# A two-layer encoder on one core: the scan's diagonal products in two column halves, one exponential per group of decays, gates per group, and priorities for the scheduler

## The chip, the cores and the metric

The kernel runs on one core of a Trainium2 chip. A core has TensorE (PE in the profile; PEld is its weight load), VectorE (DVE), ScalarE (ACT), GpSimd (POOL) and SyncE (SP, which issues the transfers). PE writes its results to PSUM tiles (128 partitions of 512 fp32 values here), from which the other engines read. The metric is the device time of one execution in microseconds; lower is better. The time before is the median of three runs, 737.57 us (736.57 to 738.35).

## What is computed

The input is x, 512 tokens of 1024 features. Layer 1 is a Mamba-2 mixer with 8 groups of 4 heads; layer 2 is differential attention with 8 heads against keys and values computed once from the residual stream; a root-mean-square norm ends it. The change lies in layer 1, whose scan is, per chunk and group:

```
acs = cumsum(a_c);  seg = acs[:, None] - acs[None, :]
decay = exp(where(causal, seg, -inf))
cb = einsum("lgn,sgn->lsg", c_c, b_c)
y_diag = einsum("lsgr,sgrp->lgrp", cb * decay, x_c)
y_off = einsum("lgn,grpn->lgrp", c_c, state) * exp(acs)
state = state * exp(acs[-1]) + einsum("lgn,lgrp->grpn", b_c, x_c * exp(acs[-1] - acs))
y = y_diag + y_off + d_skip * xs
u = y * silu(z);  u = u * rsqrt(mean(u * u) over the group) * g
x = x + u @ w_out
```

## The kernel before

All large products run as three matmuls each, of a rounded high part and the rest (`whi`, `wlo` for weights, `a_hi`, `a_lo` for activations, `yh`, `yl` for the scan's results). The weights arrive in pieces of 1 MB (`raw`); `load` issues the transfer, and the pieces of `split` turn it into `whi` on ACT and `wlo` on DVE. `fetch` lays the splits of a piece as soon as it is called, two pieces ahead of use.

Layer 1 has dense products, in the order of `order_a`: `z` (gates, four blocks of 512 features, tiles `pz`), `g` (a group's B, C and x with their convolution, tiles `pg`, `xc`), `o` (output projection, tiles `po` with `whi` and `yh`). They are written as a generator, `stream_a`; `ssd(g)` is the scan of one group and is called as soon as the dense products of that group are laid. A scheduler with a model of each instruction's time then sets the order of the instructions on every engine in layer 1, by priority and readiness; from the last rows of layer 1 on the order is that in which the code is written (`Ordered`, `T.on`), and every recorded operation has the line of that helper, L53. In layer 1 a scan's instructions therefore lie among dense matmuls wherever the scheduler put them.

The scan works on chunks of 128 tokens, NQ = 4 of them. `decays` fetches the cumulative sums of two groups in one row per head spread over all partitions (`dec`, 128 x 2048, from `acs_d`), subtracts and masks on POOL, and takes the exponentials on ACT, for the small tile `een` and for `dec` two heads at a time. Two `dec` buffers exist; `decays` for the next two groups is called within the scan of an odd group. In `ssd`, `pcb` is C times B, multiplied on DVE into `dec`; `psA` and `psB` give the states `hst`; `pyd` is the diagonal product, per chunk and head

```
T.matmul(pyd[q][:, o:o + HD], lhsT=dec[:, h, c, :], rhs=xdt[:, c, h, :], start=True, stop=True)
```

with `dec` as the 128-column stationary side and 64 columns of `xdt` as the moving side, in plain fp32. Two chunks share a PSUM tile, so a group has two batches (`pyd_0`, `pyd_1`) of eight products. `po<-hst,xc` is the part of earlier chunks. Then `dx` is summed, multiplied by the gate `zs`, squared on ACT into `tmp`, scaled on ACT by the inverse root that DVE computes (`y_y`), turned by PE (`pyt`) and split into `yh`, `yl`, which the output projection reads.

Of the kernel before, what the change touches and what calls it, by code (L numbers as in the profile page):

```python
# [9 lines left out]
F32 = mybir.dt.float32  # L10
F32R = mybir.dt.float32r
I32 = mybir.dt.int32
AF = mybir.ActivationFunctionType
ALU = mybir.AluOpType
# [3 lines left out]
P = 128  # L18
# [4 lines left out]
G = 8  # L23
R = 4
HD = 64
H = 32
NQ = 4
# [10 lines left out]

C_GA, C_GK, C_GB, C_GG, C_SG, C_DTB, C_AL, C_CB, C_CW = 0, 8, 16, 24, 40, 41, 42, 43, 75
N_PAR = 203  # L40


class Ordered:
# [18 lines left out]
def trunk(ctx, tc, x, x_t, par, w_dt, w_in, w_out, w_kvqg, w_bo, d_skip, lam_qk, fin_g, out):  # L62
    nc = tc.nc
    V, A, T = (Ordered(tc, e) for e in (nc.vector, nc.scalar, nc.tensor))
# [5 lines left out]
    small = ctx.enter_context(tc.tile_pool(name="small", bufs=2))  # L70
# [8 lines left out]
    def ss_bank(name):  # L79
        turns[0] += 1  # L80
        tag = "mm" if turns[0] % turns[1] >= 3 else "ss"
        return psum.tile([P, 512], F32, tag=tag, name=name, bufs=3 if tag == "ss" else 4)
# [14 lines left out]
    nc.scalar.dma_start(prm[:], par[:, 0:C_CB])  # L97
    prc = const.tile([P, N_PAR - C_CB], F32, name="prc")
    x_tok = res.tile([P, NT, D], F32, name="x_tok")
# [5 lines left out]
    def source(seg):  # L105
        kind, a, b = seg
        if kind == "z":
            return w_in[a * 6 + b], [prm[:, C_GA + 4 * b + i:C_GA + 4 * b + i + 1] for i in range(4)]
        if kind == "g":
            return w_in[(a // 2) * 6 + 2 + (a % 2) * 2 + b], [prm[:, C_GA + 4 * b + i:C_GA + 4 * b + i + 1] for i in range(4)]  # L110
        if kind == "o":
            return w_out[a * 2 + b], [prm[:, C_GG + 4 * a + i:C_GG + 4 * a + i + 1] for i in range(4)]
        if kind in "bc":
            return w_bo[a], None
        name = f"v{a}" if kind == "v" else a
        at = C_GK if kind in "vk" else C_GB
        return w_kvqg[[i for i in ORDER_B if i[0] not in "bc"].index(name)], [prm[:, at + i:at + i + 1] for i in range(8)]

    ready = {}
    fetched = [0]  # L120

    def load(i):

        seg = segs[i]
        src, gains = source(seg)
        nk = 8 if seg[0] in "vkqt" else 4
        w = 2048 // nk
        raw = wp.tile([P, nk, w], F32, tag="raw", name=f"raw{i}", bufs=2)
        fetched[0] += 1

        def split():

            pool, tags = (bp, ("dec", "dec")) if seg == ("o", 3, 1) else (wp, ("whi", "wlo"))
            hi, lo = (pool.tile([P, nk, w], F32R, tag=tag, name=f"{n}{i}", bufs=2) for n, tag in zip(("whi", "wlo"), tags))
            ready[seg] = (hi, lo)

            def head(k):
                if gains:
                    A.activation(hi[:, k, :], raw[:, k, :], AF.Copy, scale=gains[k])
                else:  # L140
                    A.copy(hi[:, k, :], raw[:, k, :])

            def rest(k):
                if gains:
                    V.scalar_tensor_tensor(out=lo[:, k, :], in0=raw[:, k, :], scalar=gains[k],
                                           in1=hi[:, k, :].bitcast(F32), op0=ALU.mult, op1=ALU.subtract)
                else:
                    V.tensor_tensor(out=lo[:, k, :], in0=raw[:, k, :], in1=hi[:, k, :].bitcast(F32), op=ALU.subtract)

            return [(head, rest, k) for k in range(nk)]  # L150

        if i == 0:

            nc.sync.dma_start(raw[:, 0, :], src[:, 0:w])
            for n in range(2):
                nc.sync.dma_start(xt[0][:, 0, n * 256:(n + 1) * 256], x_t[:, 0, n * 256:(n + 1) * 256])
            nc.sync.dma_start(raw[:, 1, :], src[:, w:2 * w])
            nc.sync.dma_start(xt[0][:, 1, :], x_t[:, 1, :])
            for k in range(2, 4):
                nc.sync.dma_start(raw[:, k, :], src[:, k * w:(k + 1) * w])  # L160
                nc.sync.dma_start(xt[1][:, k - 2, :], x_t[:, k, :])
            for i in range(2, 4):
                nc.sync.dma_start(xt[i], x_t[:, 2 * i:2 * i + 2, :])
            nc.sync.dma_start(prc[:], par[:, C_CB:N_PAR])
        else:
            nc.sync.dma_start(raw.rearrange("p k n -> p (k n)"), src)
        return split

    def lay(piece):
        head, rest, k = piece[:3]  # L170
        head(k)
        rest(k)

    def fetch(upto):
        while fetched[0] < min(upto, len(segs)):
            for piece in load(fetched[0])():
                lay(piece)

    def use(seg):
        fetch(segs.index(seg) + 3)  # L180
# [100 lines left out]
    def until(key):  # L281
        while key not in done:
            next(dense[0], None)
# [53 lines left out]
    bp = bctx.enter_context(tc.tile_pool(name="bp", bufs=1))  # L337
    bp2 = bctx.enter_context(tc.tile_pool(name="bp2", bufs=2))

    zt = {}  # L340
# [1 line left out]
    conv_out = {}  # L342

    def z_out(j, t, ps):
        zs = bp2.tile([P, 512], F32, tag="zs", name=f"zs{j}_{t}", bufs=6)
        A.activation(zs, ps, AF.Silu, scale=r_col[:, t:t + 1])
        zt[j, t] = zs

# [33 lines left out]
    r_col, r_row = scales("a", ss)  # L384
# [13 lines left out]
    for k in range(KD):  # L398
        w = dw[:, k].rearrange("p a b h -> p (a b h)")
# [4 lines left out]
    for c in range(NQ):  # L404
        sl, hi, lo = (slice(i * H, (i + 1) * H) for i in (c, 0, 1))
# [123 lines left out]
    bss = small.tile([P, 2, NT], F32, name="bss", bufs=1)  # L529
    decs = {}  # L530

    def decays(j):

        for g in (2 * j, 2 * j + 1):
            hs = slice(R * g, R * g + R)
            dec = bp.tile([P, R, NQ, P], F32, tag="dec", name=f"dec{g}", bufs=2)
            nc.sync.dma_start(dec.rearrange("p h c l -> p (h c l)"),
                                acs_d[hs].rearrange("h c l -> (h c l)").partition_broadcast(P))
            een = small.tile([P, R, 2], F32, tag="een", name=f"een{g}")
            GP.tensor_copy(een, dec[:, :, 1:3, P - 1])  # L540
            for h in range(R):
                GP.tensor_tensor(out=dec[:, h], in0=dec[:, h], in1=acs_tok[:, :, R * g + h].unsqueeze(2).to_broadcast([P, NQ, P]), op=ALU.subtract)
                GP.affine_select(out=dec[:, h], in_=dec[:, h], compare_op=ALU.is_ge, fill=-BIG, base=0,
                                 pattern=[[0, NQ], [1, P]], channel_multiplier=-1)
            decs[g] = (dec, een)
        for g in (2 * j, 2 * j + 1):
            dec, een = decs[g]
            A.activation(een, een, AF.Exp)
            for h in range(0, R, 2):
                A.activation(dec[:, h:h + 2], dec[:, h:h + 2], AF.Exp)  # L550

    def ssd(g):
        bc, cc, x0, x1 = conv_out.pop(g)
        xc = (x0, x1)
        dec, een = decs.pop(g)
        hs = slice(R * g, R * g + R)

        pcb = long_bank(f"pcb{g}")
# [8 lines left out]
        xdt = bp.tile([P, NQ, R, HD], F32, tag="xdt", name=f"xdt{g}")  # L567
        dx = bp.tile([P, NQ, R, HD], F32, tag="dx", name=f"dx{g}")
        for j in range(2):
            pxt = ss_bank(f"pxt{g}_{j}")  # L570
            for c in range(NQ):
# [5 lines left out]
                            in1=dsk[:, h2].unsqueeze(1).unsqueeze(3).to_broadcast([P, NQ, 2, HD]), op=ALU.mult)  # L577
# [21 lines left out]
        pyd = []  # L599
        for q in range(2):  # L600
            pyd.append(ss_bank(f"pyd{g}_{q}"))
            for c in (2 * q, 2 * q + 1):
                for h in range(R):
                    o = (c % 2) * 256 + h * HD
                    T.matmul(pyd[q][:, o:o + HD], lhsT=dec[:, h, c, :], rhs=xdt[:, c, h, :], start=True, stop=True)
            dq = dx[:, 2 * q:2 * q + 2].rearrange("p c h e -> p c (h e)")
            V.tensor_tensor(out=dq, in0=pyd[q].rearrange("p (c e) -> p c e", c=2), in1=dq, op=ALU.add)
        if g % 2 and g < G - 1:
            decays((g + 1) // 2)

        po1 = ss_bank(f"po1{g}")
        T.matmul(po1[:, 256:512], lhsT=cc[:, P:2 * P], rhs=hsf[:, 0], start=True, stop=True)
# [1 line left out]
        for c in (2, 3):  # L614
            T.matmul(po2[:, (c - 2) * 256:(c - 1) * 256], lhsT=cc[:, c * P:(c + 1) * P], rhs=hsf[:, c - 1], start=True, stop=True)
        V.tensor_tensor(out=tmp[:, 1], in0=po1[:, 256:512].rearrange("p (h e) -> p h e", e=HD),
                        in1=eacs_tok[:, 1, hs].unsqueeze(2).to_broadcast([P, R, HD]), op=ALU.mult)
        V.tensor_tensor(out=tmp[:, 2:4], in0=po2.rearrange("p (c h e) -> p c h e", h=R, e=HD),
                        in1=eacs_tok[:, 2:4, hs].unsqueeze(3).to_broadcast([P, 2, R, HD]), op=ALU.mult)
        zo = (g % 2) * 256  # L620
        u = dx.rearrange("p c h e -> p c (h e)")
        tm = tmp.rearrange("p c h e -> p c (h e)")
        for c in range(NQ):
            if c:
                GP.tensor_tensor(out=u[:, c], in0=u[:, c], in1=tm[:, c], op=ALU.add)
            V.tensor_tensor(out=u[:, c], in0=u[:, c], in1=zt[g // 2, c][:, zo:zo + 256], op=ALU.mult)
            A.activation(tm[:, c], u[:, c], AF.Square, accum_out=ss4[:, c:c + 1])
        v4 = small.tile([P, NQ], F32, tag="v4", name=f"v4{g}")
        V.tensor_scalar(out=v4, in0=ss4, scalar1=ROOT2 / 256.0, scalar2=ROOT2 * EPS, op0=ALU.mult, op1=ALU.add)
# [10 lines left out]
            V.tensor_tensor(out=yl[:, j, :], in0=pyt, in1=yh[:, j, :].bitcast(F32), op=ALU.subtract)  # L640
        yT[g] = (yh, yl)

    decays(0)
    dense[0] = stream_a()
    for g in range(G):
        until(f"g{g}")
        ssd(g)
    until("o3")


# [336 lines left out]
    h = DH - 1  # L987
# [59 lines left out]
    y, f, o, dst = half(3, 0)  # L1047
# [71 lines left out]
```

## Time and profile before

| | |
|---|---|
| median of three runs | 737.57 us |
| profiled execution | 736.51 us |
| its span | 734.7 us |
| granted TensorE clock | 0.998 |
| PE busy | 723.1 us (98%) |
| PEld busy | 605.0 us (82%) |
| DVE busy | 530.8 us (72%) |
| ACT busy | 445.3 us (61%) |
| POOL busy | 114.8 us (16%) |

Busy time is the time in which at least one instruction of the engine ran. A matmul's row shows its length from entering the array to leaving it, and matmuls overlap, so what one costs is the distance between starts. "Idle before" is the engine's idle time ahead of an instruction, put down to what ended it. The chain of work that ended last is followed back from the last instruction, and says at each moment what the end of the execution hung on; in its pieces, an ACT piece without a name is the load of a function table.

### The profile page before, as it was taken

What the parts mean: (1) busy time and instruction counts of PE and PEld (TensorE: products, weight loads), DVE (VectorE), ACT (ScalarE), POOL (GpSimd) and SP (SyncE); (2) the same over time, 40 slices, a digit from 0 to 9 for tenths busy, and PEclk for the clock granted to TensorE, in tenths of its full rate; (3) what the DMA queues carried; (4) which work ended last, traced back from release to release, by engine and by line L of the source; (5) the groups of instructions that cost most, each with busy time, mean ns of one, the idle gap of its engine ahead of it and who ended that gap; (6) DMA issues with size and microseconds to landing.
All of it is one profiled execution on the core that took longest, in us unless ns stands there. A gap on an engine that the chain in (4) does not pass through costs nothing.

```text
span 734.7 us, 10327 instructions
## 1 busy us (share of the span) xinstructions
PE 723.1 (98%) x3733; PEld 605.0 (82%) x3733; DVE 530.8 (72%) x1202; ACT 445.3 (61%) x975; POOL 114.8 (16%) x158
## 2 busy tenths in 40 slices
PE   9999999999999999999999999999999999999996
PEld 7788878888887888877888879888898898889874
DVE  5679955798568669469895655666757857785886
ACT  6849672864829356256433258766766766766566
POOL 0117231402233141150110201000000000000002
PEclk9999999999999999999999999999999999999999
DMA  8552313224132233132113220331221131122003
GB/s 314 215 193 97 128 45 116 78 95 172 59 114 65 108 115 116 58 116 102 71 58 114 87 86 8 115 115 58 65 109 57 58 116 58 58 80 93 29 1 114
DMA packets 12914, 70.83 MB, mean 96 GB/s; under 512 B 1728, under 2 KB 2496, under 8 KB 5312
## 3 DMA queue, kind: packets, MB, share of 16 engines
q1 hardware_dynamic: 12576, 69.90, 26.5%
q8 instruction: 29, 0.48, 0.3%
q10 hardware_dynamic: 288, 0.28, 0.1%
q14 instruction: 21, 0.17, 0.1%
HBM read 68.02 MB, written 2.16 MB: 96 GB/s over the span
## 4 chain that ended last, share of the span: by engine, by line
PE 86%; DVE 6%; ACT 5%; issue 1%; DMA 1%; POOL 0%; ACTq 0%; POOLq 0%; SPq 0%
PE pg L53 20%; PE po L53 13%; PE pz L53 10%; PE pt L53 7%; PE pv L53 6%; PE pq L53 6%; PE pk L53 6%; PE pyd L53 4%; PE pb L53 3%; PE sc L53 3%; PE pc L53 2%; DVE wlo L53 2%; ACT L53 1%; PE pyt L53 1%; PE pxt L53 1%
## 5 line engine op out<-in xcount | busy, mean ns | idle before, releaser
L53 DVE SCALAR_TENSOR_TENSOR wlo<-raw,prm,whi 128x512 fp32r<-128x512 f32 (+1 forms) x256 | 151.4, 640 | 49.6 <-ACT whi L53 49.2
L53 ACT ACTIVATE whi<-raw,prm 128x512 fp32r<-128x512 f32 (+1 forms) x256 | 137.1, 609 | 58.5 <-PE pz L53 12.4
L53 PE MATMUL pg<-a_hi,whi 128*128 128x512 f32 x256 | 102.4, 401 | 0.4 <-DVE xc L53 0.4
L53 PE MATMUL pg<-a_hi,wlo 128*128 128x512 f32 x256 | 102.7, 404 | 0.0
L53 PE MATMUL pg<-a_lo,whi 128*128 128x512 f32 x256 | 101.4, 397 | 0.0
L53 DVE SCALAR_TENSOR_TENSOR xc<-pg,prc,xc 128x511 f32<-128x511 f32 (+2 forms) x96 | 70.0, 743 | 4.4 <-ACT xc L53 3.6
L53 PEld LDWEIGHTS pg<-a_hi,whi 128*128 128x128 f32 x256 | 48.2, 188 | 11.4 <-issue 0.8
L53 PEld LDWEIGHTS pg<-a_hi,wlo 128*128 128x128 f32 x256 | 48.1, 188 | 11.0
L53 PEld LDWEIGHTS pg<-a_lo,whi 128*128 128x128 f32 x256 | 48.2, 188 | 10.8
L53 PE MATMUL po<-whi,yh 128*128 128x512 f32 x128 | 50.9, 400 | 0.7 <-ACT yh L53 0.6
L53 PE MATMUL po<-wlo,yh 128*128 128x512 f32 x128 | 50.9, 400 | 0.4 <-DVE wlo L53 0.4
L53 PE MATMUL pz<-wlo,a_hi 128*128 128x512 f32 x128 | 50.5, 401 | 0.0
L53 PE MATMUL pz<-whi,a_lo 128*128 128x512 f32 x128 | 50.1, 399 | 0.0
L53 PE MATMUL po<-whi,yl 128*128 128x512 f32 x128 | 49.9, 396 | 0.0
L53 PE MATMUL pz<-whi,a_hi 128*128 128x512 f32 x128 | 49.6, 400 | 0.0
L53 ACT ACT_TABLE_LOAD x33 | 42.3, 1283 | 9.5 <-DVE xc L53 7.9
L957 POOL TENSOR_TENSOR ot<-ot,fg 128x512 f32<-128x512 f32 x4 | 5.1, 1285 | 257.6 <-PE pc L53 256.4
L53 ACT ACTIVATE s<-s,mx 128x128 f32<-128x128 f32 (+3 forms) x64 | 35.6, 559 | 9.5 <-DVE mx L53 9.3
L580 POOL TENSOR_TENSOR xe<-xdt,tok 128x256 f32<-128x256 f32 x24 | 15.4, 672 | 152.5 <-DVE xdt L53 152.5
L53 DVE CUSTOM_DVE_ANT_0 s<-sc,bias 128x128 f32<-128x128 f32 (+3 forms) x64 | 29.4, 488 | 12.3 <-PE sc L53 11.9
L53 PE MATMUL pv<-whi,b_hi 128*128 128x256 f32 x128 | 36.6, 286 | 0.0
L53 ACT ACTIVATE tmp<-dx 128x256 f32<-128x256 f32 x32 | 13.1, 411 | 38.0 <-DVE dx L53 38.0
(244 smaller groups left out, 1749.1 us busy)
## 6 DMA issues: line engine op xcount, KB each, us to landing
raw<-in_w_in SPq DMA_DIRECT2D x23, 1024.0 KB, 4.9
raw<-in_w_kvqg SPq DMA_DIRECT2D x16, 1024.0 KB, 4.8
dec<-acs_d SPq DMA_DIRECT2D x8, 1024.0 KB, 4.8
raw<-in_w_out SPq DMA_DIRECT2D x8, 1024.0 KB, 4.7
raw<-in_w_bo SPq DMA_DIRECT2D x4, 1024.0 KB, 4.8
x_tok<-in_x SPq DMA_DIRECT2D x4, 512.0 KB, 9.4
out<-ot SPq DMA_DIRECT2D x7, 256.0 KB, 2.4
raw<-in_w_in SPq DMA_DIRECT2D x4, 256.0 KB, 5.4
```

What stands on the lines that cost most here:

```text
L53: i = op(*args, **kw)
L580: GP.tensor_tensor(out=xe[:, c], in0=xdt[:, c], in1=toe_tok[:, c, hs].unsqueeze(2).to_broadcast([P, R, HD]), op=ALU.mult)
L957: GP.tensor_tensor(out=o, in0=o, in1=f, op=ALU.mult)
```

## The change

The diagonal product of a chunk and head is issued as two matmuls, one for output rows 0 to 63 and one for 64 to 127, each with 64 columns of `dec` as the stationary side. `dec` and `een` become one tile of 2056 columns, whose exponential is one instruction per group; `decays` takes a list of groups. The gates are written as tiles of 256 columns, one per group. The splits that `fetch` lays, and the whole scan of the last group, are laid under `tc.high_priority()`.

```diff
+N_DEC = R * NQ * P + 2 * R
...
     def fetch(upto):
         while fetched[0] < min(upto, len(segs)):
-            for piece in load(fetched[0])():
-                lay(piece)
+            pieces_ = load(fetched[0])()
+            with tc.high_priority():
+                for piece in pieces_:
+                    lay(piece)
...
     def z_out(j, t, ps):
-        zs = bp2.tile([P, 512], F32, tag="zs", name=f"zs{j}_{t}", bufs=6)
-        A.activation(zs, ps, AF.Silu, scale=r_col[:, t:t + 1])
-        zt[j, t] = zs
+        for i in range(2):
+            zs = bp2.tile([P, 256], F32, tag="zs", name=f"zs{j}_{t}_{i}", bufs=12)
+            A.activation(zs, ps[:, i * 256:(i + 1) * 256], AF.Silu, scale=r_col[:, t:t + 1])
+            zt[2 * j + i, t] = zs
...
-    def decays(j):
-        for g in (2 * j, 2 * j + 1):
+    def decays(gs):
+        for g in gs:
...
-            dec = bp.tile([P, R, NQ, P], F32, tag="dec", name=f"dec{g}", bufs=2)
+            both = bp.tile([P, N_DEC], F32, tag="dec", name=f"dec{g}", bufs=2)
+            dec = both[:, 0:R * NQ * P].rearrange("p (h c l) -> p h c l", h=R, c=NQ)
+            een = both[:, R * NQ * P:].rearrange("p (h q) -> p h q", h=R)
...
-            een = small.tile([P, R, 2], F32, tag="een", name=f"een{g}")
...
-        for g in (2 * j, 2 * j + 1):
-            dec, een = decs[g]
-            A.activation(een, een, AF.Exp)
-            for h in range(0, R, 2):
-                A.activation(dec[:, h:h + 2], dec[:, h:h + 2], AF.Exp)
+        for g in gs:
+            A.activation(decs[g][2], decs[g][2], AF.Exp)
...
-                    T.matmul(pyd[q][:, o:o + HD], lhsT=dec[:, h, c, :], rhs=xdt[:, c, h, :], start=True, stop=True)
+                    for r in (slice(0, 64), slice(64, 128)):
+                        T.matmul(pyd[q][r, o:o + HD], lhsT=dec[:, h, c, r], rhs=xdt[:, c, h, :], start=True, stop=True)
...
-            V.tensor_tensor(out=u[:, c], in0=u[:, c], in1=zt[g // 2, c][:, zo:zo + 256], op=ALU.mult)
+            V.tensor_tensor(out=u[:, c], in0=u[:, c], in1=zt[g, c], op=ALU.mult)
...
-        ssd(g)
+        if g < G - 1:
+            ssd(g)
+        else:
+            with tc.high_priority():
+                ssd(g)
```

The scheduler orders layer 1 anew, so rows move on every engine. On PE, around the first batch of group 0, before:

```order
L53 MATMUL psA_697<-xe_688,bt_670 128x256
L53 MATMUL psB_703<-xe_688,bt_670 128x256
L53 MATMUL pyd_0_709<-xdt_672,dec_444 128x64 x8
L53 MATMUL pg_2_644<-a_hi,whi_556 128x512
L53 MATMUL pg_2_644<-a_lo,whi_556 128x512
```

and now:

```order
L55 MATMUL psA_699<-xe_690,bt_672 128x256
L55 MATMUL psB_705<-xe_690,bt_672 128x256
L55 MATMUL pyd_0_711<-xdt_674,dec_452 64x64 x16
L55 MATMUL pg_2_646<-a_hi,whi_558 128x512
L55 MATMUL pg_2_646<-a_lo,whi_558 128x512
```

Here the place is the same, and eight products of 128 output rows have become sixteen of 64; in all eight groups the two batches stay apart, with full-width matmuls between.

On ACT, between the squares of group 0 and the scaling of its `tmp`, with the exponentials of group 2 (`een`, `dec`), before:

```order
L53 ACT_TABLE_LOAD
L53 ACTIVATE een_1003<-een_1003 128x8
L53 ACTIVATE tmp_708,ss_707<-dx_673 128x256 x2
L53 ACT_TABLE_LOAD
L53 ACTIVATE xc_907<-xc_907 128x512
L53 ACTIVATE tmp_708,ss_707<-dx_673 128x256
L53 ACT_TABLE_LOAD
L53 ACTIVATE dec_1001<-dec_1001 128x1024 x2
L53 ACT_TABLE_LOAD
L53 ACTIVATE zs_0_1168<-pz_0_914,ar_col 128x512
L53 ACTIVATE tmp_708<-dx_673,y_y 128x256 x4
```

and now:

```order
L55 ACTIVATE xc_925<-xc_925 128x512
L55 ACTIVATE tmp_710,ss_709<-dx_675 128x256 x2
L55 ACT_TABLE_LOAD
L55 ACTIVATE dec_1035<-dec_1035 128x2056
L55 ACT_TABLE_LOAD
L55 ACTIVATE zs_0_0_1196<-pz_0_932,ar_col 128x256
L55 ACTIVATE zs_0_1_1198<-pz_0_932,ar_col 128x256
L55 ACTIVATE tmp_710<-dx_675,y_y 128x256 x4
```

Four table loads have become two here; in the whole program 33 have become 23.

On ACT, in the scan of the last group, from its state (`hst`) to the parts of its result (`yh`), before:

```order
L53 ACTIVATE whi_3474<-raw_3472,prm 128x512 x4
L53 COPY hst_3267<-psA_3268 128x256
L53 ACTIVATE tmp_3279,ss_3278<-dx_3244 128x256 x3
L53 ACTIVATE whi_3610<-raw_3608,prm 128x256 x2
L53 ACTIVATE tmp_3279,ss_3278<-dx_3244 128x256
L53 ACTIVATE whi_3610<-raw_3608,prm 128x256 x6
L53 ACTIVATE tmp_3279<-dx_3244,y_y 128x256 x4
L53 CAST yh_3336<-pyt_0_3338 128x512
```

and now:

```order
L55 ACTIVATE whi_3610<-raw_3608,prm 128x512 x4
L55 COPY hst_3387<-psA_3388 128x256
L55 ACTIVATE tmp_3399,ss_3398<-dx_3364 128x256 x3
L55 ACTIVATE whi_3746<-raw_3744,prm 128x256 x5
L55 ACTIVATE tmp_3399,ss_3398<-dx_3364 128x256
L55 ACTIVATE whi_3746<-raw_3744,prm 128x256 x3
L55 ACTIVATE tmp_3399<-dx_3364,y_y 128x256 x4
L55 CAST yh_3472<-pyt_0_3474 128x512
```

Three of the splits have moved ahead of the last square; their number between the third square and the scaling is the same.

More of the change, by code (lines that the diff above doesn't have):

```diff
@@ L133, in split @@
             pool, tags = (bp, ("dec", "dec")) if seg == ("o", 3, 1) else (wp, ("whi", "wlo"))
-            hi, lo = (pool.tile([P, nk, w], F32R, tag=tag, name=f"{n}{i}", bufs=2) for n, tag in zip(("whi", "wlo"), tags))
+            if pool is bp:
+                hi, lo = (pool.tile([P, N_DEC], F32R, tag=tag, name=f"{n}{i}", bufs=2)[:, 0:2048].rearrange("p (k n) -> p k n", k=nk)
+                          for n, tag in zip(("whi", "wlo"), tags))
+            else:
+                hi, lo = (pool.tile([P, nk, w], F32R, tag=tag, name=f"{n}{i}", bufs=2) for n, tag in zip(("whi", "wlo"), tags))
             ready[seg] = (hi, lo)
@@ L530, in trunk @@
     decs = {}
-    def decays(j):
-        for g in (2 * j, 2 * j + 1):
+    def decays(gs):
+        for g in gs:
             hs = slice(R * g, R * g + R)
-            dec = bp.tile([P, R, NQ, P], F32, tag="dec", name=f"dec{g}", bufs=2)
-            nc.sync.dma_start(dec.rearrange("p h c l -> p (h c l)"),
+            both = bp.tile([P, N_DEC], F32, tag="dec", name=f"dec{g}", bufs=2)
+            dec = both[:, 0:R * NQ * P].rearrange("p (h c l) -> p h c l", h=R, c=NQ)
+            een = both[:, R * NQ * P:].rearrange("p (h q) -> p h q", h=R)
+            nc.sync.dma_start(both[:, 0:R * NQ * P],
                                 acs_d[hs].rearrange("h c l -> (h c l)").partition_broadcast(P))
-            een = small.tile([P, R, 2], F32, tag="een", name=f"een{g}")
             GP.tensor_copy(een, dec[:, :, 1:3, P - 1])
@@ L544, in decays @@
                                  pattern=[[0, NQ], [1, P]], channel_multiplier=-1)
-            decs[g] = (dec, een)
-        for g in (2 * j, 2 * j + 1):
-            dec, een = decs[g]
-            A.activation(een, een, AF.Exp)
-            for h in range(0, R, 2):
-                A.activation(dec[:, h:h + 2], dec[:, h:h + 2], AF.Exp)
+            decs[g] = (dec, een, both)
+        for g in gs:
+            A.activation(decs[g][2], decs[g][2], AF.Exp)
     def ssd(g):
@@ L554, in ssd @@
         xc = (x0, x1)
-        dec, een = decs.pop(g)
+        dec, een, _ = decs.pop(g)
         hs = slice(R * g, R * g + R)
@@ L608, in ssd @@
         if g % 2 and g < G - 1:
-            decays((g + 1) // 2)
+            decays((g + 1, g + 2))
         po1 = ss_bank(f"po1{g}")
@@ L619, in ssd @@
                         in1=eacs_tok[:, 2:4, hs].unsqueeze(3).to_broadcast([P, 2, R, HD]), op=ALU.mult)
-        zo = (g % 2) * 256
         u = dx.rearrange("p c h e -> p c (h e)")
@@ L641, in ssd @@
         yT[g] = (yh, yl)
-    decays(0)
+    decays((0, 1))
     dense[0] = stream_a()
@@ L646, in trunk @@
         until(f"g{g}")
-        ssd(g)
+        if g < G - 1:
+            ssd(g)
+        else:
+            with tc.high_priority():
+                ssd(g)
     until("o3")
```

## The prediction

> **What bounds the kernel now.** I read the page first: how busy each engine is, and which engine the chain that ended last runs along.
>
> ```profile
> span 734.7 us, 10327 instructions
> PE 723.1 (98%) x3733; PEld 605.0 (82%) x3733; DVE 530.8 (72%) x1202; ACT 445.3 (61%) x975; POOL 114.8 (16%) x158
> PE 86%; DVE 6%; ACT 5%; issue 1%; DMA 1%; POOL 0%; ACTq 0%; POOLq 0%; SPq 0%
> ```
>
> PE is busy almost all the time, and 86% of the chain is PE. So time comes off in two ways only: PE's own instructions get shorter, or PE's few waits go. The profiled execution took 736.5 us for a span of 734.7, 1.1 under the median of the three runs shown (737.6); the sum below is made against 736.5 and carried to the median at the end.
>
> Next, the product that the change splits, in the view of one tile, and the chain from 70 to 130 us, where it lies on the path.
>
> ```profile
> L53 PEld LDWEIGHTS pyd<-xdt,dec x256: 187/192/192, 76.5 to 415.9; 128*128 128x128 f32 x128
> L53 PE MATMUL pyd<-xdt,dec x256: 217/275/275, 76.7 to 416.0; 128*128 128x64 f32 x128
> ...
> 75.31 0.43 PE psA L53 x2
> ...
> 76.83 1.73 PE pyd L53 x16
> 78.56 4.95 PE pg L53 x21
> 83.51 1.75 PE pyd L53 x16
> ```
>
> Each fp32 product is two passes (128 products, 256 loads and 256 matmuls). A batch of eight products, 16 passes, holds PE for 1.73 us, so a pass costs 0.108 us; the 275 ns of the tile's row are a length in the pipe, not a price. There are 16 batches: 16 x 1.73 = 27.7 us of the span. What sets 0.108? The moving side has 64 columns. A psA pass moves 256 columns of fp32 and costs 0.43/2 = 0.215, so 64 columns at that rate are 0.054. The stationary side has 128 columns in either case. The score matmuls of the second layer show this apart, in a type of one pass:
>
> ```profile
> 542.51 0.27 PE L53 MATMUL sc<-k,q_lo 128*128 128x128 f32 x1
> 542.63 0.27 PE L53 MATMUL sc<-k,q 128*128 128x128 f32 x1
> 542.74 0.27 PE L53 MATMUL sc<-k,q_lo 128*128 128x128 f32 x1
> ...
> 548.98 0.28 PE L53 MATMUL sc<-k,q_lo 128*128 128x256 f32 x1
> 549.10 0.28 PE L53 MATMUL sc<-k,q 128*128 128x256 f32 x1
> 549.22 0.28 PE L53 MATMUL sc<-k,q_lo 128*128 128x256 f32 x1
> ```
>
> The first number is the start. Passes of 256 columns start 0.12 apart (half of the 4.95/21 = 0.236 of the 512-column passes pg above), but passes of 128 columns still start 0.11 to 0.12 apart and not 0.06. What they share is the 128-column weight load. So a pass with few columns is paced by its load at about 0.11, and half of PE's time in pyd is spent loading.
>
> Last, PE's waits, and what ACT does ahead of one of them.
>
> ```profile
> PEld pyt L53 <- ACT tmp L53: 4.4, 13, 1.1
> PEld po L53 <- ACT yh L53: 0.8, 1, 0.8
> ...
> 99.27 1.28 ACT L53
> 100.55 0.01 issue
> 100.56 2.01 ACT dec L53 x2
> 102.57 0.02 issue
> 102.59 1.28 ACT L53
> ...
> 104.47 1.71 ACT tmp L53 x4
> 106.17 0.04 issue
> 106.22 0.55 PE pyt L53 x3
> ```
>
> The transposes pyt wait for the scaled tmp, 4.4 us in 13 places over all groups. At 98 to 106 us the chain leaves PE: ACT loads a function table (the unnamed 1.28), takes the decays' exponentials, loads a table back, and only then scales tmp.
>
> **The change part by part.**
>
> *Column halves.* 128 products become 256 of 64 output rows, each two passes: 512 loads of 64 columns and 512 matmuls in place of 256 and 256. No row of this trace has a tile narrower than 128 columns, so the price of a pair of half passes is bounded. From below: both halves side by side, 0.054, the moving side's rate. From above: each half as dear as a whole one, 2 x 0.108 = 0.216. Between them stands 0.108: loads of 64 columns at half the time, one after the other. I take 0.060, next to the moving rate, because the halves have different output partitions and different weights and no value passes between them; the 0.006 on top is my allowance, since the rows show no fixed cost per pass. 256 x (0.108 - 0.060) = 12.3 us less. At 0.054 it is 13.8 less, at 0.108 nothing, at 0.216 27.7 more.
>
> The Trainium skill ("TensorEngine Tiling (Array Packing)", Key Properties) says that different tiles can load weights and multiply in parallel, which by itself would bring the pair to 0.054; the trace before has no tiles to show it.
>
> *Entering and leaving the halves.* There are 16 batches, so 32 changes of tile shape, each beside a full-width product. No row shows one. Nearest is the first full-width pass behind a batch:
>
> ```profile
> 76.67 1.89 PE L53 MATMUL pyd<-xdt,dec 128*128 128x64 f32 x16
> 78.37 0.48 PE L53 MATMUL pg<-a_hi,whi 128*128 128x512 f32 x1
> 78.68 0.40 PE L53 MATMUL pg<-a_lo,whi 128*128 128x512 f32 x1
> 78.92 0.40 PE L53 MATMUL pg<-a_hi,wlo 128*128 128x512 f32 x1
> ```
>
> It holds PE 0.31 against 0.24 for the next: 0.07 for a load that nothing long enough hid. If the array had to empty at each change, a pass's length less its moving time (0.275 - 0.054 = 0.22) and a load (0.11) would show: 0.33. So a change costs 0 to 0.33, 0 to 10.6 us in all. I take 0.15, nearer to the row than to the bound: 32 x 0.15 = 4.8 us more.
>
> The Trainium skill, in the same page and section, also says that a change of tiling mode drains the engine; by that, with the 0.33 of an emptied array, this term would be 10.6 and the two terms together -1.7.
>
> *Exponentials in one instruction, gates in halves, and the order.* These rows are ACT's.
>
> ```profile
> L53 ACT ACT_TABLE_LOAD x33 | 42.3, 1283 | 9.5 <-DVE xc L53 7.9 <-PEq L1112 1.2
> L53 ACT ACTIVATE dec<-dec 128x1024 f32<-128x1024 f32 x16 | 16.6, 1055 | 1.1 <-POOL dec L543 1.0
> L53 ACT ACTIVATE tmp<-dx 128x256 f32<-128x256 f32 x32 | 13.1, 411 | 38.0 <-DVE dx L53 38.0
> L53 ACT ACTIVATE zs<-pz,ar_col 128x512 f32<-128x512 f32 x16 | 10.6, 678 | 1.4 <-PE pz L53 1.3
> ```
>
> One exponential over 2056 columns instead of two over 1024 is within 0.2 us of the 2.01 that two take. What changes is the order: no een stands alone before a second table, and the built program holds 23 table loads where the old one holds 33, so 10 x 1.28 = 12.8 us of ACT go. Gates in halves add 16 instructions: two of some 0.5 (between the 0.41 of a 128x256 and the 0.68) for one of 0.68, 16 x 0.3 = 5 us more on ACT. Both lie beside PE, with ACT 61% busy; if that cover went, they would net to 8 us less on ACT. They count where PE waits for ACT. The splits laid ahead of other work and the last scan's priority likewise move only who goes first on ACT and DVE; no transfer is added, and from the last row sums of the first layer on, ACT and DVE have the same rows as before. So the gain here is bounded by the waits of pyt and po, 4.4 + 0.8 = 5.2. The exponentials with their tables no longer stand between the squares and the scaling at 98 to 106 us in parts, but one load pair still does, and the last scan still has eight splits between its squares and its scaling. I take 2.0 less, 0 to 5.2, and as a new wait at worst 4 more: the scan's steps have less PE work beside them when batches are shorter.
>
> Sum: -12.3 + 4.8 - 2.0 = -9.5; 736.5 - 9.5 = 727.0, and against the median 737.6 - 9.5 = 728.1. I say 728.
>
> **The rivals.**
>
> *Loads in turn, and the changes of shape paid (slower).* The two halves use all 128 rows of the array and their loads go through one port, one after the other. For it: every load in this trace covers 128 columns and paces the short passes, and nothing shows two loads at once. Against it: the halves are independent. Then a pair costs 0.108, the gain is nothing and the changes remain: 0 + 4.8 - 2.0 = +2.8, 740; at 0.22 a change, +5, 743. It decides from a pair price of 0.097 on, where 256 x 0.011 = 2.8 no longer pays. The Trainium skill ("TensorE: Matmul & The Clock Gate", the mechanism of Part 3) sees a load overlap a running matmul only when the row group differs, and column halves share all rows: by that rule this rival holds.
>
> *The halves do nothing.* Loads in turn, and a change of shape as cheap as 0: only the 2.0 of waits go, or none of them: 736 to 738.
>
> *The gain given back as waits.* Halves at 0.060, but pyt and po wait longer, since PE reaches them 1.5 us sooner in each group (2 x (1.73 - 0.96)): +4 in place of -2.0 gives -3.5, 734. Against it stands DVE at 72%.
>
> *Each half as dear as a whole.* +27.7 + 4.8 - 2.0 = +30.5, 768. For it: the 0.11 could be the floor of any pass and not the time of its load, since every load in this trace has 128 columns and no row can part the two. Against it stands only that a load half as wide moves half as much.
>
> **How the numbers follow.** Side by side with net gain 0.58; loads in turn with a price 0.20; nothing 0.09; given back 0.08; as dear as two 0.05. The low end is the pair at 0.054 (-13.8), changes at 0.05 (1.6) and most of the waits gone (-4.4): 737.6 - 16.6 = 721. The high end is 743, loads in turn at 0.22 a change. Only the last case and tails lie outside. The likeliest case alone spans 721 to 735. 0.2% (1.5 us) is about what a measurement of this kernel can tell from no change. Faster: 0.58, most of given back (0.06) and a little of nothing (0.02) make 0.66; same: the rest of nothing and a little of the others, 0.08; slower: 0.26.
>
> **What would show it.** The chain's pyd pieces, 16 passes in 1.73 now: 32 half passes in about 1.0 if side by side, 1.7 if in turn, 3.5 if each is whole. The first full-width pass behind a batch: 0.31 now, 0.4 to 0.65 if the array empties. Table loads: 23. PE's waits for tmp: under 4.4 in all. Wrong would make it, above all, a pair price that stays at 0.108, or a price of shape changes at its upper bound.

## The result and the profile after

The changed kernel takes 729.12 us in the median of four runs (727.83 to 730.13) against 737.11 before (four runs, the three given above and one more); the ratio is 0.9887, 95% interval 0.9874 to 0.9900. The profiled execution has a span of 727.0 us, 7.7 under that of before. These are the same rows of the page of the changed kernel: span, busy time, the chain by engine.

```profile
span 727.0 us, 10819 instructions
PE 713.5 (98%) x3989; PEld 593.1 (82%) x3989; DVE 528.0 (73%) x1202; ACT 433.7 (60%) x965; POOL 117.7 (16%) x158
PE 90%; DVE 7%; ACT 1%; issue 1%; POOL 0%; ACTq 0%; DVEq 0%; POOLq 0%
```

PE has 256 matmuls more and is busy 9.6 us less. The chain hangs on PE as before, and ACT's share of it has gone from 5% to 1%.

The split product, in the groups of its tile (the load above, the pass below; the mean ns of one is among the columns), then in the chain around group 0 (start, length, engine, tile), then on PE's timeline:

```profile
L55 PEld LDWEIGHTS pyd<-xdt,dec x512: 132/138/138, 78.2 to 408.3; 128*64 128x64 f32 x171
L55 PE MATMUL pyd<-xdt,dec x512: 222/222/270, 78.2 to 408.4; 128*64 128x64 f32 x171
```

```profile
77.88 0.43 PE psB L55 x2
78.31 1.08 PE pyd L55 x32
79.39 5.10 PE pg L55 x21
84.49 1.08 PE pyd L55 x32
```

```profile
77.72 0.59 PE L55 MATMUL psB<-xe,bt 128*128 128x256 f32 x2
78.24 1.15 PE L55 MATMUL pyd<-xdt,dec 128*64 128x64 f32 x32
79.33 0.50 PE L55 MATMUL pg<-a_hi,whi 128*128 128x512 f32 x1
79.66 0.40 PE L55 MATMUL pg<-a_lo,whi 128*128 128x512 f32 x1
```

Twice the instructions take 1.08 us in place of 1.73. Within a batch a half pass starts 0.030 us after the last one on average (from the starts of all 16 batches), so a pair of halves costs 0.060. The single starts show the pairs: the second half starts 0.007 after the first, and the next pair 0.052 after that, so in the steady part a pair costs 0.0585. Whole passes started 0.112 apart there. The rest of the average is at the ends of a batch: the second pair comes 0.05 late, and from the last half pass to the first full-width one 0.15 go by. That first pg pass holds PE for 0.33, where it held it for 0.31 before, and not for the 0.4 to 0.65 that the prediction gives an emptied array. At the entry, psB's second pass is followed 0.09 later than its own 0.215.

The waits of PE and of its weight loads that changed most (who waited for whom, us in total, times, longest), and ACT's rows that changed:

```profile
PE pg L55 <- DVE y_c L55: 1.5, 1, 1.5
...
PE po L55 <- DVE xc L55: 0.8, 1, 0.8
PE pyt L55 <- ACT tmp L55: 0.7, 1, 0.7
PE pxt L55 <- ACT xc L55: 0.6, 1, 0.6
...
PEld pyt L55 <- ACT tmp L55: 1.8, 4, 1.2
```

```profile
L55 ACT ACT_TABLE_LOAD x23 | 29.5, 1283 | 6.8 <-DVE xc L55 3.0 <-DVE y_c L55 2.4 <-PEq L1126 1.2
...
L55 ACT ACTIVATE dec<-dec 128x2056 f32<-128x2056 f32 x8 | 15.4, 1924 | 7.7 <-POOL dec L554 7.6
...
L55 ACT ACTIVATE zs<-pz,ar_col 128x256 f32<-128x256 f32 x32 | 12.9, 472 | 0.1
```

The waits of pyt for the scaled tmp fell from 4.4 us in 13 places to 1.8 in 4. Others came: before a pg matmul (1.5), a po (0.8), a pxt (0.6). The largest is late because of DVE, as the chain around it shows.

```profile
322.92 0.61 DVE pg L55
323.53 0.34 DVE v L55
...
323.89 0.98 DVE y_i L55
...
324.90 0.99 DVE y_y L55
...
325.91 0.56 DVE y_c L55
...
329.16 1.32 DVE xc L55 x2
330.47 0.08 DVE y_c L55
...
330.62 2.57 PE pg L55 x10
```

DVE works off a scan's root (v, y_i, y_y, y_c) between the steps of a convolution (pg, xc), and the pg matmul waits for them. The wait is put down to y_c because it ended last; a pg matmul reads no y_c, so what it needed was more likely the xc step just ahead of it, which the root had made late.

To tell the two causes apart I added up, for every kernel, the distances between starts on PE. "Batches" is what the pyd batches hold, from the first start to the next full-width matmul, with what the matmul before and the one behind take beyond their usual distance. "Waits" is what all other distances exceed the usual ones (0.233 for 512 columns, 0.117 for 256, 0.215 for 256 in fp32, 0.109 for 128), the start of the program included and the 7.0 to 7.1 us behind the last product left out.

| kernel | median us | ratio to before, interval | span | batches | waits |
|---|---|---|---|---|---|
| before | 737.1 | | 734.7 | 28.6 | 10.9 |
| changed | 729.1 | 0.9887 (0.9874 to 0.9900) | 727.0 | 20.5 | 11.2 |
| e1 whole products | 743.5 | 1.0085 (1.0071 to 1.0099) | 742.0 | 28.6 | 18.1 |
| e2 halves alone | 745.0 | 1.0098 (1.0080 to 1.0117) | 740.4 | 20.5 | 24.7 |
| e3 halves by side | 742.3 | 1.0079 (1.0063 to 1.0096) | 738.3 | 32.5 | 10.6 |
| e4 joined by the scheduler | 733.3 | 0.9950 (0.9936 to 0.9963) | 730.7 | 26.1 | 9.3 |
| e5 joined and kept | 722.8 | 0.9806 (0.9791 to 0.9821) | 720.9 | 17.7 | 7.9 |
| e6 quarters | 734.8 | 0.9971 (0.9959 to 0.9982) | 732.0 | 19.7 | 17.0 |
| e7 no scan priority | 731.4 | 0.9927 (0.9906 to 0.9948) | 728.3 | 20.5 | 12.5 |
| e8 no priority | 732.1 | 0.9937 (0.9919 to 0.9954) | 730.8 | 20.5 | 15.0 |
| e9 two exponentials | 730.6 | 0.9912 (0.9891 to 0.9932) | 727.9 | 20.5 | 12.1 |
| e10 wide gates | 739.0 | 1.0030 (1.0016 to 1.0044) | 737.6 | 20.8 | 21.5 |

All other products are the same in every kernel, so the spans differ as the two columns do: 734.7 - 727.0 = 7.7 is 8.1 from the batches less 0.3 more of waits. "Waits" is what is left over, and holds more than idle time. In five kernels PE worked for a while at a granted clock of 0.50 (half clock, below) in the middle of the program, and I put the passes' excess there at about 2.8 us of the column in e1, 3.0 in e2, 1.5 in e6, 2.7 in e8 and 3.9 in e10. The other seven have no such stretch before their last product. The five with it are the five with the most waits; the last section returns to this.

### The profile page after: what moved, and what is told of

Read it like the earlier page. It is cut to its first block, busy times and chain, and to the rows that moved or that the text cites. A ratio compares the mean times of both kernels' runs of the same rounds, so it can differ in the third digit from the quotient of the medians.

```text
span 727.0 us, 10819 instructions
## 1 busy us (share of the span) xinstructions
PE 713.5 (98%) x3989; PEld 593.1 (82%) x3989; DVE 528.0 (73%) x1202; ACT 433.7 (60%) x965; POOL 117.7 (16%) x158
## 4 chain that ended last, share of the span: by engine, by line
PE 90%; DVE 7%; ACT 1%; issue 1%; POOL 0%; ACTq 0%; DVEq 0%; POOLq 0%
PE pg L55 21%; PE po L55 14%; PE pz L55 12%; PE pt L55 7%; PE pv L55 6%; PE pq L55 6%; PE pk L55 6%; PE pb L55 3%; PE sc L55 3%; PE pyd L55 2%; PE pc L55 2%; DVE wlo L55 2%; DVE xc L55 2%; PE pyt L55 1%; PE pxt L55 1%; PE psA L55 1%
## 5 line engine op out<-in xcount | busy, mean ns | idle before, releaser
L55 ACT ACTIVATE xc<-pg,prc 128x512 f32<-128x512 f32 x32 | 24.6, 773 | 26.6 <-DVE pg L55 26.5
L589 POOL TENSOR_TENSOR xe<-xdt,tok 128x256 f32<-128x256 f32 x24 | 17.3, 749 | 139.6 <-DVE xdt L55 139.6
L55 ACT ACTIVATE xc<-xc 128x512 f32<-128x512 f32 x32 | 20.0, 629 | 28.3 <-DVE xc L55 28.2
```

The source lines that it names most:

```text
L55: i = op(*args, **kw)
L589: GP.tensor_tensor(out=xe[:, c], in0=xdt[:, c], in1=toe_tok[:, c, hs].unsqueeze(2).to_broadcast([P, R, HD]), op=ALU.mult)
```

## The experiments

**e1: the products whole again.**

```diff
-                    for r in (slice(0, 64), slice(64, 128)):
-                        T.matmul(pyd[q][r, o:o + HD], lhsT=dec[:, h, c, r], rhs=xdt[:, c, h, :], start=True, stop=True)
+                    T.matmul(pyd[q][:, o:o + HD], lhsT=dec[:, h, c, :], rhs=xdt[:, c, h, :], start=True, stop=True)
```

> The changed kernel with the diagonal products whole again (128 columns of dec stationary), all its other edits kept. Theory (the halves carry the gain: 16 batches of 1.08 us go back to 1.72, entries and exits of 0.25 a batch go): +8.1 us on the changed kernel, about 737, a batch of 16 passes at 1.70 to 1.73. Rival (the new order and the fewer table loads carry it): 729 to 731.

743.46 us, 6 us over what the theory had, and the rival's 729 to 731 fails too. The batches are back at 28.6, 8.1 more, as expected; a batch in the chain of this kernel:

```profile
77.15 0.43 PE psB L55 x2
77.58 1.73 PE pyd L55 x16
79.31 4.49 PE pg L55 x19
```

But the waits rose by 6.9 as well, some 2.8 of it at half clock. The scheduler orders layer 1 anew when the products change, and this order is worse. So the other edits without the halves made a kernel slower than before.

**e2: the kernel before with the halves alone.**

> The kernel before with the column halves alone. Theory (halves carry all, the other edits about nothing): 737.1 - 8.1 = 729, with 1.5 us either way for waits, since the scheduler orders layer 1 anew; a batch at 1.08. Rival (the halves pay only together with the other edits' order): 733 or more.

744.95 us: the theory's 729 failed. The batches fell by 8.1 to 20.5, the same as in the changed kernel; the waits went from 10.9 to 24.7. One of them, from this kernel's waits, then on PE's timeline:

```profile
PE po L53 <- DVE x_tok L53: 6.3, 1, 6.3
```

```profile
229.97 0.40 PE L53 MATMUL po<-whi,yl 128*128 128x512 f32 x1
236.69 0.79 PE L53 MATMUL po<-whi,yh 128*128 128x512 f32 x1 [6.33 <-DVE x_tok L53]
237.29 0.63 PE L53 MATMUL po<-wlo,yh 128*128 128x512 f32 x1
```

The gain of the halves is in the trace in full, and one order of the rest takes it back nearly twice over. The rival's 733 or more came true, and by the waits, not by the price of a half. So neither e1 nor e2 shows a gain by itself; that the halves carry it rests on the batches, which fall by the same 8.1 in both comparisons.

**e3: the same halves, sixteen of one side and then sixteen of the other.**

```diff
-            for c in (2 * q, 2 * q + 1):
-                for h in range(R):
-                    o = (c % 2) * 256 + h * HD
-                    for r in (slice(0, 64), slice(64, 128)):
+            for r in (slice(0, 64), slice(64, 128)):
+                for c in (2 * q, 2 * q + 1):
+                    for h in range(R):
+                        o = (c % 2) * 256 + h * HD
```

> The changed kernel with the loop over halves outermost in a batch: sixteen passes on the lower 64 output rows, then sixteen on the upper, so neighbours in the row use the same half of the array. Same products, same number of instructions. Theory (two halves run side by side only when neighbours are on different halves of the array; one half alone is held to its moving rate, 0.054 a pass): 32 x 0.054 + 0.12 = 1.85 a batch, 16 x 0.77 = +12.3 us on the changed kernel, about 741. Rival (a load and a pass of half width are simply cheaper, 0.030, wherever they go): a batch stays at 1.08 and the kernel at 729.

742.28 us, the theory's 741 within its scatter. The chain of this kernel:

```profile
77.45 1.83 PE pyd L55 x32
...
84.37 1.83 PE pyd L55 x32
```

1.83 a batch (1.85 expected), 12.0 more over all batches, and the order around it is nearly that of the changed kernel, with waits of 10.6. On one side half passes start 0.058 to 0.059 apart, as far as whole pairs do in the changed kernel. The average is 0.054, because at the change of side three pairs start 0.004 to 0.006 apart; the trace does not say why these ran together. Same instructions, same load widths: only that neighbours use the two sides in turn makes two half passes start in the time of one. This shows that the two halves run side by side, loads included, and that a smaller load by itself brings nothing here (1.83 against 1.73 for whole products).

**e4: both batches of a group behind each other, by PSUM tile.**

```diff
+        pyd = [ss_bank(f"pyd{g}_0"), long_bank(f"pyd{g}_1")]
         for q in range(2):
-            pyd.append(ss_bank(f"pyd{g}_{q}"))
             for c in (2 * q, 2 * q + 1):
...
+        for q in range(2):
             dq = dx[:, 2 * q:2 * q + 2].rearrange("p c h e -> p c (h e)")
```

> The changed kernel with the second batch of a group in the PSUM tile of pcb, so that both batches stand behind each other on PE: 16 changes of tile shape fewer. Theory (a change costs 0.125 us): -2.0 us, 727, where no new wait comes; a double batch of 64 half passes at 0.030 = 1.92 + 0.12. Rival (the cost at the ends of a batch is the pipe's and not the shape's, or the sums that follow come late): 729 or more.

733.31 us. The kernel was not what the expectation assumed: the scheduler issued products as soon as a head of dec was ready, and PE's chain shows them in pieces among psA and psB:

```profile
75.16 0.27 PE pyd L55 x4
75.43 0.63 PE psA L55 x2
...
76.94 0.27 PE pyd L55 x4
77.21 0.63 PE psB L55 x2
77.84 1.55 PE pyd L55 x46
```

That is 29 visits to the halves instead of 16 (a visit is an unbroken row of half passes on PE); 5.6 us more in the batches, 0.43 for each extra visit (two psA passes take 0.63 among them, 0.43 elsewhere). It measured the price it was to save, from the other side. The rival's 729 or more came true for a third reason.

**e5: joined, and the sixteen products kept in their order.**

```diff
+        pyd = [long_bank(f"pyd{g}_0"), ss_bank(f"pyd{g}_1")]
+        T.on = True
         for q in range(2):
...
                         T.matmul(pyd[q][r, o:o + HD], lhsT=dec[:, h, c, r], rhs=xdt[:, c, h, :], start=True, stop=True)
+        T.on = False
+        for q in range(2):
```

> The changed kernel with the first batch in the PSUM tile of pcb (free only when all four heads of dec are multiplied) and the sixteen products of a group kept in their order on PE, so that the 64 half passes of a group stand together: 8 visits to the halves instead of 16. Theory (a visit costs 0.26 us net, two changes of shape at 0.13): 8 x 0.26 = 2.1 us less PE time in the batches and their ends; 727 if the other waits stay. Rival (a visit's price is in the tail of the last pass and grows with the batch): no change in the batches, 729.

722.76 us, the fastest here: 0.9806 of before (0.9791 to 0.9821), with the changed kernel at 0.9887. Its chain (the span is 720.9):

```profile
77.69 0.43 PE psB L55 x2
78.12 2.02 PE pyd L55 x64
80.14 1.13 PE pg L55 x4
```

8 visits of 2.02 in place of 16 of 1.08: the batches with their ends go from 20.5 to 17.7, 2.8 us for 8 visits fewer, 0.35 a visit. That bears the theory out (2.1 expected), and the rival falls. The other 3.3 us are waits, 7.9 in place of 11.2; they come with the new order and are not credited to the joining. That is why it came out 4 us below the theory's 727.

**e6: quarters of 32 rows** (four slices in the loop over r).

> The changed kernel with each product in four parts of 32 output rows. Theory A (the moving side at 0.054 is the bound, any number of column parts runs side by side): four quarter passes in 0.054 to 0.060, a batch of 64 in 1.0 to 1.1, 729. Theory B (the 0.030 from one half pass to the next is a least distance between passes): 64 x 0.030 + 0.12 = 2.04 a batch, 16 x 0.96 = +15 us, about 744.

734.82 us: neither number. The batch itself decides clearly. Its row in the chain of this kernel:

```profile
78.65 1.03 PE pyd L55 x64
```

64 quarter passes in 1.03, 0.014 apart, four in 0.056. So theory A holds for the array: the 0.060 of a pair is the moving side's, not a least distance between passes nor a load's length, since loads of half the columns leave it where it was. Four parts bring next to nothing over two because the moving side was already the bound. The span is 5.0 over the changed kernel's: 0.8 less in the batches, 5.8 more in waits (17.0), one of 3.5 before a pcb matmul.

**e7 and e8: no priority for the last scan; none at all.**

```diff
-        if g < G - 1:
-            ssd(g)
-        else:
-            with tc.high_priority():
-                ssd(g)
+        ssd(g)
```

(e8 also lays the splits in `fetch` without priority.)

> The changed kernel without the priority of the last scan. Theory (the scheduler's order around 360 to 430 us decides PE's waits there, now 1.0 before a po matmul at 361 and 0.9 + 0.7 at 420 to 424): a change of under 1 us either way, 728 to 730. Rival (the priority holds back the splits and causes the 1.0): 728 or less, with that wait gone.

> The changed kernel without either priority (splits, last scan). Theory (the priorities are what keeps PE's waits at 12.9 us in all, where halves alone on the kernel before had 26.3): waits of 20 us or more, 735 or more. Rival (the waits come from the exponentials and their table loads, which stay as in the changed kernel): 729 to 731.

731.44 and 732.05 us: e7 lies 1.4 over its theory and e8 well under its own, 1 over its rival. The batches are unchanged. Without the scan's priority the wait before the last pyt grows from 0.9 to 1.9 and the wait at 361 stays, so the priority did not cause that one; the effect, 1.3 of span, is at the edge of what these runs can tell. Without both, waits are 15.0, not 20, so the priorities are not what keeps the kernel from e2's 24.7 (26.3 in the expectation, which used an earlier count, with 12.9 for the 11.2). They are worth some 2 to 3 us here, but e8's 15.0 hold 2.7 of half clock behind a wait that e7 has as well, without half clock.

**e9: the exponentials as before, in the tiles of the change.**

```diff
-            A.activation(decs[g][2], decs[g][2], AF.Exp)
+            dec, een, both = decs[g]
+            A.activation(een, een, AF.Exp)
+            for h in range(0, R, 2):
+                A.activation(dec[:, h:h + 2], dec[:, h:h + 2], AF.Exp)
```

> The changed kernel with the exponentials as before, een alone and dec in two, in the tiles of the change: 31 table loads instead of 23. Theory (the new waits of PE come from the order that the scheduler happens to find and not from ACT's work; the pyt waits at 98 to 106 us come back): 8 x 1.28 = 10 us more on ACT, of which PE sees 1 to 3 in new waits: 730 to 732. Rival (ACT's time is hidden beside PE): 729.

730.55 us, waits 12.1, span 0.9 longer. The intervals of this kernel and the changed one overlap, so between the theory's 730 and the rival's 729 it does not decide; it shows that eight table loads more (31 in its trace) cost at most 1 or 2 us in the order they brought.

**e10: gates in tiles of 512, read in halves.**

> The changed kernel with the gates in tiles of 512 as before, read in halves. Theory (5 us less of ACT work, all beside PE; what moves is the order): the halves as in the changed kernel, waits of PE between 9 and 19 us in all, 726 to 735. Rival (the gates per group pay by themselves, as half the tile comes free a group sooner): 731 or more with waits for the gates before pz.

738.96 us, beyond the theory's 735. The largest waits of this kernel:

```profile
PE po L55 <- DVE xc L55: 4.3, 1, 4.3
PE pg L55 <- DVE xc L55: 2.7, 1, 2.7
```

They are DVE's convolution steps. In its list of waits a gate ends one only, 0.2 us of a weight load for pg; a wait of 1.5 before pz is put down to DVE. So the rival's mechanism is not there either, though its 731 or more came true: the edit that takes ACT work away made the kernel 10 us slower by another order, some 3.9 of it at half clock. (The batches are 20.8 because one is issued in two parts.)

## Why the prediction was right

The mechanism was right: the halves run side by side, changing over costs a few us, and what is left is 8.1 us of PE's own time.

*Column halves, -12.3.* 512 half passes at 0.030 are 15.4, against 27.7: 12.3. The 0.060 for a pair was taken by reasoning from the moving rate; e3 and e6 show that this is what it is. The rival "loads in turn" is excluded by the pair's 0.060, "as dear as two" by the 1.08.

The Trainium skill ("TensorEngine Tiling (Array Packing)", Key Properties) has tiles load and multiply in parallel; the trace agrees, 0.060 a pair and 0.056 for four quarters. The Trainium skill's rule on row groups ("TensorE: Matmul & The Clock Gate", the mechanism of Part 3), by which loads of column halves would not overlap running matmuls, does not hold here: loads 138 ns long start 7 and 52 ns apart in turn, while passes of the other half run.

*Changes of shape, +4.8.* Batches and ends beyond the passes themselves are 20.5 - 15.4 = 5.1 now and 28.6 - 27.7 = 0.9 before: 4.2, or 0.13 for each of 32 changes, with 0.15 taken. How the 8.1 divides depends on the count. By the steady distances, 0.112 a pass before and 0.0585 a pair now, the passes fall by 13.7 and the ends grow by 5.6, which is 0.35 for each of 16 visits. e5, which takes 8 visits away, measures the same 0.35, and e4, which adds 13, measures 0.43. The sum does not depend on the count: -8.1, with -7.5 forecast. That the price is one of visits is shown.

*Waits, -2.0.* This is the term that was mis-sized: it measured +0.3. Its first half was right (pyt's waits went from 4.4 to 1.8, table loads from 33 to 23). What it missed is that the scheduler's new order brings waits of its own, for DVE, of the same size. The bound of 4 us for new waits was also too small for the step as a whole: among kernels with the same batches, to 0.3 us, the waits run from 11.2 to 24.7 (e2, e7 to e10 and the changed one). The changed kernel has the least of these six, and nothing in the prediction could tell that it would; that 729.1 came so near to 728 is in this part luck. The rival "the gain given back as waits" is what e2 and e10 did, mostly by waits for DVE ahead of po and pg.

*ACT.* Tables -12.8 and gates +5 were to net -8; ACT fell 11.6. The gates cost 12.9 - 10.6 = 2.3 in busy time: two of 0.47 for one of 0.68 would be 4.2 more over all, but the two overlap on ACT (32 of 0.47 are 15.1 us, busy for 12.9). The exponentials took 1.2 less.

## What to carry to other kernels

A product with few moving columns (64 here) is paced by its 128-column weight load, 0.112 a pass; cut in two column halves that alternate on PE, it falls to its moving rate, 0.0585 a pair, and it must be in turn, not side after side. Each visit to the halves costs 0.35 to 0.43 us here, so keep such products together, if need be by fixing their order. Where a scheduler orders the work, judge an edit by PE's instructions and by PE's waits separately: here the waits moved by up to 14 us for edits that touched PE not at all or for the better.

## What the runs showed of the hardware

*A long wait can cost twice.* These are stretches of e2 around its 6.3 us wait (length, PE, PEld, DVE, ACT, POOL busy, then granted clock, DMA share, GB/s):

```profile
225.00:230.00 5.00, 5.00 (x23) 3.97 (x22) 5.00 (x7) 4.99 (x9) 4.60 (x6) 1.00 0.28 80
...
236.00:240.00 4.00, 3.31 (x8) 2.63 (x9) 3.90 (x12) 2.02 (x3) 0.00 (x0) 0.50 0.69 262
```

After the wait the granted clock was 0.50 until 240.5 us, and 512-column passes started 0.42 apart (237.29 and 237.71). The length of the wait does not decide it alone. In e1 a wait of 2.3 us at 141 was followed by 3.4 us at half clock, in e3 one of 2.4 us at 337 by none. In e8 and e7 PE waits at the same place, 1.8 us (e8) and 1.9 us (e7) before the last pyt and 0.8 and 0.7 behind it. These are the 6.5 us that follow, of e8 and then of e7:

```profile
424.00:430.50 6.50, 6.04 (x15) 4.53 (x16) 1.29 (x2) 1.07 (x2) 0.00 (x0) 0.50 0.02 6
```

```profile
424.00:430.50 6.50, 5.93 (x26) 4.64 (x26) 1.55 (x3) 1.07 (x2) 0.00 (x0) 1.00 0.07 28
```

PE issues 15 passes at half clock where it issues 26 at the full one. All stretches at half clock before the last product are 3.41 or 6.83 us long in these traces. The Trainium skill ("TensorE: Matmul & The Clock Gate", What's actually happening) explains this by a free-running window of activity of 3.4 us, with half clock after at least one idle window; the traces agree with the length, but the waits of 1.8 and 2.3 us are shorter than such a window. So a wait of some 2 us can cost up to 3 us more behind it, or nothing; no trace here tells beforehand which.

*POOL slows small DVE instructions.* An instruction of POOL in the changed kernel, on its timeline:

```profile
320.94 4.92 POOL L553 TENSOR_TENSOR dec<-dec,tok 128x512 f32<-128x512 f32 x4
```

DVE's steps of a scan's root on 128x4 values on the timeline of the same kernel, two that begin within that instruction (320.94 to 325.86) and two later ones that are clear of POOL:

```profile
323.89 0.97 DVE L55 TENSOR_SCALAR y_i<-v 128x4 int32<-128x4 int32 x1
324.90 0.98 DVE L55 TENSOR_SCALAR y_y<-y_i 128x4 int32<-128x4 int32 x1
...
420.31 0.16 DVE L55 TENSOR_TENSOR y_c<-y_y,v 128x4 f32<-128x4 f32 x1
420.51 0.16 DVE L55 TENSOR_TENSOR y_c<-y_c,y_y 128x4 f32<-128x4 f32 x1
```

In the changed kernel 14 of the 80 such steps start while POOL works on dec and take 0.55 in the median, the 65 clear of POOL 0.16; before it was 20 of 80, and in e5 none. That this made the 1.5 us wait at 329 is argued from the chain shown above, not tried. The Trainium skill ("SBUF — State Buffer", Who interferes with whom) has DVE and GpSimd share a port pair as an exclusive lock; the lengths agree, since each of the 14 ends 0.01 to 0.03 us after the POOL instruction in which it began.
